# Moving three of the four token sums of each FFN into the output projection before it, and taking two gate columns fewer as whole products

## The chip, the cores and the metric

One core of a Trainium2 chip runs the whole program. The time is device time in microseconds of one execution, told as the median of several. The engines are TensorE (PE; its weight loads are PEld), VectorE (DVE), ScalarE (ACT), GpSimd (POOL) and SyncE (SP, which here only issues transfers). The granted TensorE clock in the profiled execution is 0.998.

## The reference

A decoder trunk with two layers over 512 tokens of width 1024, all in float32. Layer 0 mixes with a gated DeltaNet, layer 1 with sliding-window attention; both also attend into 256 memory tokens. What matters here is the end of each layer:

```
x = x + concat(mix_out, mem_o) @ w_out[layer]          # 1024 x 1024
gu = rms_norm(x, ln_ffn) @ w_gate_up[layer]            # 1024 x 5632
x = x + (silu(gu[:, :2816]) * gu[:, 2816:]) @ w_down[layer]
```

## The kernel before

**Tiles.** x is held transposed, as eight tiles x[0..7] of 128 features by 512 tokens. Each float32 operand is split in a high and a low part (`split`: ACT copies the high part, DVE subtracts it from the original), and a product is three matmuls, high by high, high by low and low by high (`mm3`). A weight column of 128 outputs is a 128x1024 tile: `load` (SP, 512 KB, two buffers `wraw`), then `weight` splits it into `whi` (ACT) and `wlo` (DVE), three buffers each. A whole column (`project`) is 8 x 3 matmuls of 128x512.

**Output projection** (`output`). Eight rows, one for each x[m]. Behind the last matmul of a row come, on DVE, `x <- pj,x` (add from PSUM), `l <- x,gains,h` (low part of the scaled row, after ACT's high part `h`) and `sqa <- sqa,sq` (sum of squares, after ACT's square). `opened_rows` gives a function `part(m, *ks)` that splits the weights of row m at its first call and runs some of its blocks k. The first three rows run in pieces beside the end of the mixer (`rest`); the other five follow one another in whole. In layer 0 the rows use blocks 6 and 7 (the memory heads `mq0`, `mq1`, held in the pool of layer 0) first.

**FFN** (`ffn`). A pair of columns for 512 tokens is taken in seven products of quarter size in place of eight (`quarters`: halves of the 1024 features against halves of the tokens, 4 x 3 matmuls of 128x256 each, 84 for a pair against 48 of 128x512 in two whole columns). It needs sums of weights and sums of activations. The weights: `s1` and `s3` are loaded by SP (lines 1112 and 1113) and a second quarter is added to each by an accumulating transfer issued by POOL (1114, 1115); the first column of the pair comes by `load`, the fourth quarter by line 1117. The activations: `token_sums(j)` for j = 0..3 combines x[j] and x[j+4]: on DVE one 128x256 `fs <- x,gains`, four 128x256 `fu <- x,...`, and the low halves of two 128x512 splits `T <- fu,T` (high halves on ACT). Products t1 to t4 of every pair need the sums of all four j; products 11, 21 and 22 need only h.

The four sums need all of x, so the first four gate columns of an FFN are taken whole while they are formed: gate 0, gate 1 (with the norm's reciprocal root between its matmuls), sums 0 and 1, gate 2, sums 2, gate 3, sums 3. Then follow pairs (`begin`): up 0-1, up 2-3, gate 4-5, up 4-5 and so on. The split halves of a product lie in a ring of six places that is cut out of the three `whi`/`wlo` buffers.

**Order.** The program text sets what depends on what. A planner lays out each engine's queue when the program is built: among the instructions that it holds to be ready, the one that the text emits first goes first. So an instruction of later text can stand in a queue before one of earlier text that is held to wait, and a later-emitted one that is ready stays behind an earlier-emitted one that is ready too. On the chip each queue runs in order. A tile that reuses a buffer waits for the last reader of the tile before it.

**Pools.** `fp` holds the FFN's tiles on the right side of the memory, where the mixer's pools were before; among them `T` (eight buffers, token sums), `ws` (s1 and s3), `fs`, `fu`. `xp` holds x and, under the tag `sq`, two buffers for squares.

Of the kernel before, what the change touches and what calls it, by code (L numbers as in the profile page):

```python
# [9 lines left out]
F32 = mybir.dt.float32  # L10
F32R = mybir.dt.float32r
# [7 lines left out]
P = 128  # L19
T = 512  # L20
D = 1024
KD = D // P
# [17 lines left out]
G_MIX, G_FFN, G_MEM, G_KV, G_FIN = (0, 8), (16, 24), 32, 40, 48  # L40
# [10 lines left out]
INV_FREQ = [float.fromhex(s) for s in (  # L51
    "0x1.0000000000000p+0", "0x1.8d275e0000000p-3", "0x1.3411900000000p-5", "0x1.ddee9c0000000p-8",
    "0x1.72ba440000000p-10", "0x1.1f91f00000000p-12", "0x1.be21880000000p-15", "0x1.5a0f4e0000000p-17")]
SHUFFLE = list(range(8, 16)) + list(range(8)) + list(range(16, 32))


# [31 lines left out]
class Builder:  # L88
    def __init__(self, tc, a):
        self.tc, self.nc, self.a = tc, tc.nc, a  # L90
        self.n = 0
        self.table, self.table_ins, self.table_users = None, None, []
        self.locked, self.latest = False, None


    def t(self, pool, shape, dtype=F32, tag=None, bufs=None, name=None):
# [158 lines left out]
    def build(self):  # L255
        tc, nc, a = self.tc, self.nc, self.a
        with ExitStack() as st:
            opened = lambda name, **kw: tc.tile_pool(name=name, bufs=1, reuse_waits="tile", **kw)
            pool = lambda name, **kw: st.enter_context(opened(name, **kw))
            cp = pool("const")  # L260
            self.wpool, self.apool = pool("w"), pool("acta")
            self.dpool = pool("scratch", space=DRAM)
            self.load_constants(cp)
            pool("edge", side="right").tile([P, 8], F32, name="edge")
            self.weng = nc.vector
            with opened("layer0", side="right") as self.mpool:
                with self.banks(pj=3, g=2, sc=3):
                    with opened("early", side="right") as ep:
                        self.mem_and_norm(ep)
                        self.gates(ep)  # L270
                    with opened("gdn", side="right") as gp:
                        mix, part = self.gdn(gp)
                    self.bpool, xp = pool("actb"), pool("x")
                    self.x = [self.t(xp, [P, T], F32, f"x{k}") for k in range(KD)]
                    for k in range(KD):
                        nc.sync.dma_start(self.x[k], a["xT"][:, k, :])
# [7 lines left out]
                    h = self.output(xp, 0, part, self.bpool, rest)  # L284
            with opened("ffn0", side="right") as fp, self.banks(pj=2, g=6):
                self.ffn(fp, xp, 0, h, self.apool, rope=True)
            with self.banks(pj=2, qk=1, pt=4):
                with opened("swa", side="right") as sp:
                    mix, rest = self.swa(sp, xp)
                    h = self.output(xp, 1, self.opened_rows(1, mix), self.apool, rest)  # L290
            with opened("ffn1", side="right") as fp, self.banks(pj=2, g=6):
                self.ffn(fp, xp, 1, h, self.bpool)

    def load_constants(self, cp):
        nc, a = self.nc, self.a
# [607 lines left out]
        return steps  # L903


    def row_bank(self, m):

        if m % 3 < 2:
            return self.bank("pj")
        if "g" in self.pbufs:  # L910
            return self.bank("g")
        return self.bank("qk", [P, 2, T])[:, 0]

    def opened_rows(self, layer, mix):

        rows = {}
# [12 lines left out]
    def output(self, xp, layer, part, hpool, ahead=None):  # L929

        nc, a = self.nc, self.a
        self.weng = nc.vector
        h = []
        self.acc = None

        def row(m, *ks):
            ps = part(m, *ks)
# [8 lines left out]
        if ahead is not None:  # L946
            ahead(row)
        for m in range(len(h), KD):
            row(m, 6, 7, 0, 1, 2, 3, 4, 5)
        return h  # L950

    def ffn(self, fp, xp, layer, h, apool, rope=False):

        nc, a = self.nc, self.a
        self.exact(xp)
        acc = self.acc
        acts, sums, open_pairs, places = [], [], [], []

        col = lambda f, up: a["wgu"][layer, 2 * f + up]

# [2 lines left out]
            self.use(SILU_SIN)  # L963

        def gate(f, between=None):
            return self.project(col(f, 0), h, "pj", between=between)

        def gated(ps):
            g = self.t(fp, [P, T], F32, "fg", 4)
            self.tt(nc.vector, g, ps, self.rstd, ALU.mult)  # L970
            self.fn(g, g, AF.Silu)
            return g
# [12 lines left out]
            places.append(places.pop(0))  # L985
            return places[-1]

        def begin(f, up, by, tag, bufs, then):

            o = [self.t(fp, [P, T], F32, tag, bufs) for _ in range(2)]  # L990
            steps = self.quarters(fp, [col(f + i, up) for i in range(2)], sums, by, o, ring)
# [60 lines left out]
        if tail < KD:  # L1052

            parts = (slice(0, T // 2), slice(T // 2, T))
            own = dict(pool=fp, tags=("T", "T"), bufs=8)
            w = {m: [down(m, j, n, **(own if m == KD - 1 else {})) for j, n in ((0, 6), (6, half - 6))] for m in range(tail, KD)}
            outs = [[self.t(fp, [P, D], F32, "T", 8).rearrange("p (k t) -> p k t", k=4) for _ in range(2)] for t in parts]
# [18 lines left out]
            for (ps, r), o, t in zip(ends, outs, parts):  # L1076
                self.store(ps, r, o, t)

    def token_sums(self, fp, layer, j, h):


        q = T // 2
# [6 lines left out]
        c = self.t(fp, [P, q], F32, "fs", 3)  # L1089
        raw = [self.t(fp, [P, T], F32, "fu", 3) for _ in range(2)]  # L1090
# [14 lines left out]
    def quarters(self, fp, src, sums, by, u, ring):  # L1105

        nc = self.nc
        q = T // 2
# [5 lines left out]
        nc.gpsimd.dma_start(s1, a22, accum_op=ALU.add)  # L1114
# [274 lines left out]
```

## Time and profile before

| | us |
|---|---|
| median of 3 runs | 1140.61 (1140.49 to 1140.86) |
| the profiled execution | 1140.3 |
| its span, first to last instruction | 1138.5 |
| PE busy | 1121.8 (99%) |
| DVE busy | 841.5 (74%) |
| ACT busy | 634.0 (56%) |
| POOL busy | 86.1 (8%) |

The span has 19673 instructions. A row of a timeline gives start, duration, engine, line, operation, what is written from what, and in brackets the idle time ahead of it with what ended that. A row of the chain gives start, duration and the work that stands on the path to the end of the span. A row of a window table gives a stretch, its length, and the busy time of each engine in it.

### The profile page before, as it was taken

What the parts mean: (1) busy time and instruction counts of PE and PEld (TensorE: products, weight loads), DVE (VectorE), ACT (ScalarE), POOL (GpSimd) and SP (SyncE); (2) the same over time, 40 slices, a digit from 0 to 9 for tenths busy, and PEclk for the clock granted to TensorE, in tenths of its full rate; (3) what the DMA queues carried; (4) which work ended last, traced back from release to release, by engine and by line L of the source; (5) the groups of instructions that cost most, each with busy time, mean ns of one, the idle gap of its engine ahead of it and who ended that gap; (6) DMA issues with size and microseconds to landing.
All of it is one profiled execution on the core that took longest, in us unless ns stands there. A gap on an engine that the chain in (4) does not pass through costs nothing.

```text
span 1138.5 us, 19673 instructions
## 1 busy us (share of the span) xinstructions
PE 1121.8 (99%) x7476; PEld 992.8 (87%) x7476; DVE 841.5 (74%) x1590; ACT 634.0 (56%) x1278; POOL 86.1 (8%) x97
## 2 busy tenths in 40 slices
PE   7999999999999999999999999999999999999997
PEld 6888887887899998899998888888999988999986
DVE  6754887776789987389876768959799843899743
ACT  7569572365566653256653656855566522566524
POOL 0120000000101100011100000010011100111000
PEclk9999999999999999999999999999999999999999
DMA  8433342324668744567723421153477833677232
GB/s 311 119 123 114 119 107 99 95 91 149 188 143 190 189 124 130 158 144 188 186 71 93 135 74 57 42 130 126 121 187 177 202 98 107 149 190 182 70 95 95
DMA packets 73971, 152.76 MB, mean 134 GB/s; under 512 B 17756, under 2 KB 18420, under 8 KB 73876
## 3 DMA queue, kind: packets, MB, share of 16 engines
q1 hardware_dynamic: 62356, 130.52, 37.4%
q0 software_dynamic: 11520, 20.98, 11.9%
q8 instruction: 59, 0.97, 0.3%
q14 instruction: 36, 0.29, 0.1%
HBM read 144.51 MB, written 6.96 MB: 133 GB/s over the span
## 4 chain that ended last, share of the span: by engine, by line
PE 95%; DVE 2%; ACT 1%; DMA 1%; issue 1%; SPq 0%; DVEq 0%; ACTq 0%
PE pj L154 48%; PE g L154 37%; PE sc L154 6%; PE pt L154 2%; PE qk L154 2%; PE pt L168 1%; PE g L168 1%; DVE wlo L171 1%; DMA wraw<-in_wmk 1%; ACT whi L148 0%; ACT sm L142 0%; SPq L329 0%; DVE x L171 0%; DVE l L174 0%; DVE stats L836 0%
## 5 line engine op out<-in xcount | busy, mean ns | idle before, releaser
L148 ACT ACTIVATE whi<-wraw 128x512 fp32r<-128x512 f32 (+2 forms) x331 | 243.6, 746 | 249.1 <-PE pj L154 160.1
L171 DVE TENSOR_TENSOR wlo<-wraw,whi 128x512 fp32r<-128x512 f32 (+2 forms) x331 | 273.0, 835 | 109.1 <-ACT whi L148 102.7
L154 PE MATMUL pj<-h,whi 128*128 128x512 f32 (+1 forms) x676 | 265.5, 393 | 0.1
L154 PE MATMUL pj<-l,whi 128*128 128x512 f32 (+1 forms) x676 | 263.7, 390 | 0.0
L154 PE MATMUL pj<-h,wlo 128*128 128x512 f32 (+1 forms) x676 | 263.2, 390 | 0.0
L154 PE MATMUL g<-T,whi 128*128 128x256 f32 x1280 | 228.1, 278 | 0.2
L154 PEld LDWEIGHTS g<-T,whi 128*128 128x128 f32 x1280 | 194.7, 188 | 1.8 <-DVE fu L174 1.8
L154 PE MATMUL g<-T,wlo 128*128 128x256 f32 x640 | 177.8, 278 | 0.0
L154 PEld LDWEIGHTS pj<-h,whi 128*128 128x128 f32 x676 | 126.9, 188 | 28.3 <-issue 3.5
L154 PEld LDWEIGHTS pj<-h,wlo 128*128 128x128 f32 x676 | 127.0, 188 | 25.9 <-DVE wlo L171 0.4
L154 PEld LDWEIGHTS pj<-l,whi 128*128 128x128 f32 x676 | 127.1, 188 | 24.7 <-DVE l L171 0.4
L154 PE MATMUL g<-h,whi 128*128 128x256 f32 (+1 forms) x492 | 138.4, 281 | 0.0
L154 PE MATMUL g<-h,wlo 128*128 128x256 f32 (+1 forms) x492 | 138.0, 280 | 0.0
L154 PE MATMUL g<-l,whi 128*128 128x256 f32 (+1 forms) x492 | 138.0, 280 | 0.0
L154 PEld LDWEIGHTS g<-T,wlo 128*128 128x128 f32 x640 | 120.1, 188 | 0.0
L154 PEld LDWEIGHTS g<-l,whi 128*128 128x128 f32 x492 | 92.3, 188 | 0.8 <-issue 0.2
L154 PEld LDWEIGHTS g<-h,whi 128*128 128x128 f32 x492 | 92.3, 188 | 0.8 <-issue 0.2
L154 PEld LDWEIGHTS g<-h,wlo 128*128 128x128 f32 x492 | 92.3, 188 | 0.5
L1114 POOL DMA_DIRECT2D ws<-in_wgu x40 | 35.5, 887 | 700.7 <-DMA ws<-in_wgu 278.2
L148 ACT ACTIVATE whi<-ws 128x512 fp32r<-128x512 f32 x80 | 50.5, 631 | 48.9 <-PE g L154 38.4
L171 DVE TENSOR_TENSOR wlo<-ws,whi 128x512 fp32r<-128x512 f32 x80 | 54.7, 684 | 4.5 <-ACT whi L148 4.5
L1115 POOL DMA_DIRECT2D ws<-in_wgu x40 | 35.1, 877 | 213.4 <-DVE wlo L171 73.5
(383 smaller groups left out, 1637.4 us busy)
## 6 DMA issues: line engine op xcount, KB each, us to landing
wraw<-in_wgu SPq DMA_DIRECT2D x48, 512.0 KB, 4.2
ws<-in_wgu SPq DMA_DIRECT2D x80, 256.0 KB, 3.5
ws<-in_wgu POOLq DMA_DIRECT2D x80, 256.0 KB, 4.8
wraw<-in_wdn SPq DMA_DIRECT2D x48, 384.0 KB, 3.1
wraw<-in_win SPq DMA_DIRECT2D x26, 512.0 KB, 3.6
wraw<-in_wgu SPq DMA_DIRECT2D x40, 256.0 KB, 4.4
wraw<-in_wout SPq DMA_DIRECT2D x16, 512.0 KB, 3.6
wraw<-in_wdn SPq DMA_DIRECT2D x16, 256.0 KB, 2.7
```

Of the source, the lines that this page charges most:

```text
L148: self.copied = self.nc.scalar.activation(out, in_, AF.Copy, **kw).ins
L154: return self.chained(self.nc.tensor.matmul(out, lhsT, rhs, start=start, stop=stop, skip_group_check=more).ins)
L168: return self.chained(self.nc.tensor.transpose(out, in_, self.ident[:k, :k]).ins)
L171: return eng.tensor_tensor(out=out, in0=a, in1=b, op=op).ins
L1114: nc.gpsimd.dma_start(s1, a22, accum_op=ALU.add)
L1115: nc.gpsimd.dma_start(s3, a21, accum_op=ALU.add)
```

## The change

It has five parts.

1. The rows of the output projection are taken in the order 0, 4, 1, 5, 2, 6, 3, 7 (`TURN`), so that x[j] and x[j+4] come one behind the other. r counts in this order; the gate columns run through the blocks of h in the same order.
2. Behind the rows r = 3, 4 and 6 the weights of row r + 1 are opened (`part(r + 1)` with no blocks: load and split only), and then the token sums 0, 1 and 2 are emitted. Their temporaries come from a pool `turn` that lives in `output` and from the tag `sq` of `xp`; their results lie in a pool `tok` that lives on (six buffers `T`), and `fp` keeps two `T` for the fourth sum. The `T` tiles of the last FFN's end are taken from both.
3. Only gate 0 and gate 1 are whole columns. Sum 3 is emitted behind them. Gate 2-3 becomes a pair in quarters.
4. s1, s3 and the fourth quarter of the first pair (`summed`) are emitted before the norm's results are used, and the load of that pair's first column is held behind them in SP's queue (`behind`, an order without a wait).
5. `token_sums` gets its temporaries and pool from the caller; `quarters` takes quarters already loaded.

```diff
+TURN = (0, 4, 1, 5, 2, 6, 3, 7)
     def load(self, src, pool=None, bufs=2):
-        self.nc.sync.dma_start(raw, src)
+        ins = self.nc.sync.dma_start(raw, src).ins
+        if self.behind is not None:
+            self.nosync(ins, self.behind)
+            self.behind = None
...
+                    self.tok = pool("tok")
...
-        def part(m, *ks):
-            if m not in rows:
-                rows[m] = self.weight(self.a["wout"][layer, m]), self.row_bank(m), []
-            w, ps, done = rows[m]
+        def part(r, *ks):
+            if r not in rows:
+                rows[r] = self.weight(self.a["wout"][layer, TURN[r]]), []
+            if not ks:
+                return
+            if r not in banks:
+                banks[r] = self.row_bank(r)
+            (w, done), ps = rows[r], banks[r]
...
+        def work():
+            return self.t(xp, [P, T], F32, "sq", 2)[:, :T // 2], [self.t(tp, [P, T], F32, "raw", 2) for _ in range(2)]
+
+        def row(r, *ks):
+            ps = part(r, *ks)
             if ps is None:
                 return
+            m = TURN[r]
             self.tt(nc.vector, self.x[m], ps, self.x[m], ALU.add)
-            hl = self.pair(hpool)
-            self.split_gain(self.x[m], self.gain(G_FFN[layer], m), *hl)
-            h.append(hl)
+            h[m] = self.pair(hpool)
+            self.split_gain(self.x[m], self.gain(G_FFN[layer], m), *h[m])
             self.acc = self.accumulate(xp, self.acc, self.x[m])
+            if r in (3, 4, 6):
+                part(r + 1)
+                sums.append(self.token_sums(layer, len(sums), h, work, self.tok, 6))
...
         def gate(f, between=None):
-            return self.project(col(f, 0), h, "pj", between=between)
+            return self.project(col(f, 0), h, "pj", TURN, between=between)
...
-            whole = []
+            whole, loaded = [], None
             if f0 == 0:
                 two = [gate(0), gate(1, {1: [norm]})]
+                loaded = self.summed(fp, columns(0, 1))
+                self.behind = self.quarter
                 whole += [gated(ps) for ps in two]
-                sums += [self.token_sums(fp, layer, f, h) for f in range(2)]
-                for f in (2, 3):
-                    whole.append(gated(gate(f)))
-                    sums.append(self.token_sums(fp, layer, f, h))
+                sums.append(self.token_sums(layer, 3, h, work, fp, 2))
...
-                begin(f, 1, g, "fu", 3, put)
+                begin(f, 1, g, "fu", 3, put, loaded)
+                loaded = None
...
-        hl = [self.t(fp, [P, D], F32R, "T", 8) for _ in range(2)]
+        hl = [self.t(pool, [P, D], F32R, "T", bufs) for _ in range(2)]
...
+    def summed(self, fp, src):
         (a11, a12), (a21, a22) = ([c[:, :T], c[:, T:]] for c in src)
-        a1 = self.load(src[0])
         s1, s3 = (self.t(fp, [P, T], F32, "ws", 4) for _ in range(2))
         nc.sync.dma_start(s1, a21)
         nc.sync.dma_start(s3, a11)
         nc.gpsimd.dma_start(s1, a22, accum_op=ALU.add)
         nc.gpsimd.dma_start(s3, a21, accum_op=ALU.add)
         last = self.t(fp, [P, T], F32, "wraw", 2)
-        nc.sync.dma_start(last, a22)
+        self.quarter = nc.sync.dma_start(last, a22).ins
+        return s1, s3, last
+
+    def quarters(self, fp, src, sums, by, u, ring, loaded=None):
+        a1 = self.load(src[0])
+        s1, s3, last = loaded or self.summed(fp, src)
```

More of the change, by code (lines that the diff above doesn't have):

```diff
@@ L92, in __init__ @@
         self.table, self.table_ins, self.table_users = None, None, []
-        self.locked, self.latest = False, None
+        self.locked, self.latest, self.behind = False, None, None
     def t(self, pool, shape, dtype=F32, tag=None, bufs=None, name=None):
@@ L282, in rest @@
                                 row(m, k)
-                    h = self.output(xp, 0, part, self.bpool, rest)
+                    h, sums = self.output(xp, 0, part, self.bpool, rest)
             with opened("ffn0", side="right") as fp, self.banks(pj=2, g=6):
-                self.ffn(fp, xp, 0, h, self.apool, rope=True)
+                self.ffn(fp, xp, 0, h, sums, self.apool, rope=True)
             with self.banks(pj=2, qk=1, pt=4):
@@ L289, in build @@
                     mix, rest = self.swa(sp, xp)
-                    h = self.output(xp, 1, self.opened_rows(1, mix), self.apool, rest)
+                    h, sums = self.output(xp, 1, self.opened_rows(1, mix), self.apool, rest)
             with opened("ffn1", side="right") as fp, self.banks(pj=2, g=6):
-                self.ffn(fp, xp, 1, h, self.bpool)
+                self.ffn(fp, xp, 1, h, sums, self.bpool)
     def load_constants(self, cp):
@@ L914, in opened_rows @@
     def opened_rows(self, layer, mix):
-        rows = {}
-        def part(m, *ks):
-            if m not in rows:
-                rows[m] = self.weight(self.a["wout"][layer, m]), self.row_bank(m), []
-            w, ps, done = rows[m]
+        rows, banks = {}, {}
+        def part(r, *ks):
[6 more added lines that the diff above has]
+            (w, done), ps = rows[r], banks[r]
             for k in ks:
@@ L932, in output, with ffn @@
         self.weng = nc.vector
-        h = []
+        h, sums = {}, []
         self.acc = None
-        def row(m, *ks):
-            ps = part(m, *ks)
+        def work():
+            return self.t(xp, [P, T], F32, "sq", 2)[:, :T // 2], [self.t(tp, [P, T], F32, "raw", 2) for _ in range(2)]
+        def row(r, *ks):
+            ps = part(r, *ks)
             if ps is None:
                 return
+            m = TURN[r]
             self.tt(nc.vector, self.x[m], ps, self.x[m], ALU.add)
-            hl = self.pair(hpool)
-            self.split_gain(self.x[m], self.gain(G_FFN[layer], m), *hl)
-            h.append(hl)
+            h[m] = self.pair(hpool)
+            self.split_gain(self.x[m], self.gain(G_FFN[layer], m), *h[m])
             self.acc = self.accumulate(xp, self.acc, self.x[m])
[L946 to L952, printed above, removed]
+            if r in (3, 4, 6):
+                part(r + 1)
+                sums.append(self.token_sums(layer, len(sums), h, work, self.tok, 6))
+        with self.tc.tile_pool(name="turn", bufs=1, reuse_waits="tile") as tp:
+            if ahead is not None:
+                ahead(row)
+            for r in range(len(h), KD):
+                row(r, 6, 7, 0, 1, 2, 3, 4, 5)
+        return h, sums
+    def ffn(self, fp, xp, layer, h, sums, apool, rope=False):
         nc, a = self.nc, self.a
@@ L956, in ffn @@
         acc = self.acc
-        acts, sums, open_pairs, places = [], [], [], []
+        acts, open_pairs, places = [], [], []
         col = lambda f, up: a["wgu"][layer, 2 * f + up]
@@ L965, in gate, with work @@
         def gate(f, between=None):
-            return self.project(col(f, 0), h, "pj", between=between)
+            return self.project(col(f, 0), h, "pj", TURN, between=between)
+        def work():
+            return self.t(fp, [P, T // 2], F32, "fs", 3), [self.t(fp, [P, T], F32, "fu", 3) for _ in range(2)]
         def gated(ps):
@@ L986, in ring, with columns, begin @@
             return places[-1]
-        def begin(f, up, by, tag, bufs, then):
+        def columns(f, up):
+            return [col(f + i, up) for i in range(2)]
+        def begin(f, up, by, tag, bufs, then, loaded=None):
             o = [self.t(fp, [P, T], F32, tag, bufs) for _ in range(2)]
-            steps = self.quarters(fp, [col(f + i, up) for i in range(2)], sums, by, o, ring)
+            steps = self.quarters(fp, columns(f, up), sums, by, o, ring, loaded)
             next(steps)
@@ L1077, in ffn, with token_sums @@
                 self.store(ps, r, o, t)
-    def token_sums(self, fp, layer, j, h):
+    def token_sums(self, layer, j, h, work, pool, bufs):
         q = T // 2
@@ L1088, in token_sums @@
         x0, x1 = self.x[j], self.x[j + 4]
-        c = self.t(fp, [P, q], F32, "fs", 3)
-        raw = [self.t(fp, [P, T], F32, "fu", 3) for _ in range(2)]
+        c, raw = work()
         t = [x[:, i * q:(i + 1) * q] for x in raw for i in range(2)]
```

13 lines of the change are left out of this document (7 added, 6 removed).

## The prediction

> **What bounds the kernel now.** First the page: its head, the busy line of TensorE, and the shares of the chain of work that ended last.
>
> ```profile
> span 1138.5 us, 19673 instructions
> PE 1121.8 (99%) x7476; PEld 992.8 (87%) x7476; DVE 841.5 (74%) x1590; ACT 634.0 (56%) x1278; POOL 86.1 (8%) x97
> ...
> PE 95%; DVE 2%; ACT 1%; DMA 1%; issue 1%; SPq 0%; DVEq 0%; ACTq 0%
> ```
>
> TensorE is on 95% of the chain, so time comes only from fewer or cheaper matmuls, or from its pauses. Then the chain in order of time, which gives the pace of both kinds of matmul; "x66" counts them.
>
> ```profile
> 312.79 14.98 PE pj L154 x66
> 327.77 96.60 PE g L154 x828
> ...
> 772.18 5.44 PE qk L154 x24
> ...
> 795.76 15.00 PE pj L154 x66
> 810.76 96.60 PE g L154 x828
> ```
>
> A 128x512 matmul of a whole column takes 14.98 / 66 = 0.227 us (a column or row of 24: 5.44), a 128x256 one of the quarters 96.60 / 828 = 0.1167 us. The row at 772.18 is r5 of layer 1. Both stretches lie on the chain without a gap, in both layers: the whole gates run straight into the quarters.
>
> Third, the windows cut at the rows and columns of layer 0: r4, r5, r6, r7, and gate 1 (gate 0 fills the 5.44 us between).
>
> ```profile
> core 0: us, PE busy (x) PEld busy (x) DVE busy (x) ACT busy (x) POOL busy (x), PEclk, DMA share, GB/s
> 283.93:289.21 5.28, 5.28 (x23) 4.40 (x24) 3.60 (x5) 3.25 (x4) 0.00 (x0) 1.00 0.59 189
> 289.21:294.65 5.44, 5.44 (x25) 4.50 (x25) 3.87 (x5) 2.34 (x4) 0.00 (x0) 1.00 0.47 127
> 294.65:300.10 5.45, 5.45 (x25) 4.51 (x25) 3.18 (x4) 2.20 (x4) 0.00 (x0) 1.00 0.60 195
> 300.10:305.54 5.44, 5.44 (x25) 4.50 (x25) 5.19 (x10) 2.31 (x4) 1.01 (x1) 1.00 0.50 147
> ...
> 310.98:316.89 5.91, 5.91 (x27) 4.87 (x27) 5.91 (x11) 4.58 (x6) 1.25 (x2) 1.00 0.99 177
> ```
>
> TensorE never pauses here. VectorE is the nearest rival: in the four rows it idles 1.68 + 1.57 + 2.27 + 0.25 = 5.77 us. Whether the moved sums fit there decides the result.
>
> **The change part by part.**
>
> *Gates 2 and 3 in quarters.* Removed on TensorE: 48 x 0.227 = 10.90 us. Added: 84 x 0.1167 = 9.80. Gain 1.10 us for each FFN, less some 0.02 for the hand-over of a pair: 1.07, and **2.14 us for both**. The pair also moves 5 x 256 KB + 512 KB where two columns moved 1 MB, by two more SP issues and two more POOL issues, and VectorE work of the kind of the ten pairs of this window:
>
> ```profile
> 327.77:424.37 96.60, 96.60 (x830) 96.60 (x829) 86.42 (x156) 61.27 (x118) 13.00 (x16) 1.00 0.71 170
> ```
>
> 86.42 of 96.60 us on VectorE, 61.27 on ScalarE, 0.71 of the DMA engines: an eleventh pair like these is hidden, zero. If VectorE were the limit there, a pair would cost 8.64 us of it, which TensorE's 9.66 still covers.
>
> *Three token sums beside the rows.* Pace of VectorE by starts of neighbours, layer 0:
>
> ```profile
> 276.26 0.69 DVE L171 TENSOR_TENSOR x<-pj,x 128x512 f32<-128x512 f32 x1 [2.24 <-PE pj L154]
> 277.13 1.22 DVE L171 TENSOR_TENSOR wlo<-wraw,whi 128x1024 fp32r<-128x1024 f32 x1 [0.18 <-ACT whi L148]
> 278.27 0.68 DVE L171 TENSOR_TENSOR x<-pj,x 128x512 f32<-128x512 f32 x1
> 278.87 0.74 DVE L174 SCALAR_TENSOR_TENSOR l<-x,gains,h 128x512 fp32r<-128x512 f32 x1
> 279.53 0.68 DVE L171 TENSOR_TENSOR x<-g,x 128x512 f32<-128x512 f32 x1
> ...
> 283.89 0.69 DVE L171 TENSOR_TENSOR x<-pj,x 128x512 f32<-128x512 f32 x1
> 285.01 1.23 DVE L171 TENSOR_TENSOR wlo<-wraw,whi 128x1024 fp32r<-128x1024 f32 x1 [0.43 <-ACT whi L148]
> ...
> 305.16 0.48 DVE L174 SCALAR_TENSOR_TENSOR fu<-x,gains,fs 128x256 f32<-128x256 f32 x1
> 305.56 0.48 DVE L174 SCALAR_TENSOR_TENSOR fu<-x,eps,fu 128x256 f32<-128x256 f32 x1
> ...
> 308.21 0.68 DVE L171 TENSOR_TENSOR sqa<-sqa,sq 128x512 f32<-128x512 f32 x1
> 308.82 0.68 DVE L171 TENSOR_TENSOR T<-fu,T 128x512 fp32r<-128x512 f32 x1
> 309.42 0.48 DVE L174 SCALAR_TENSOR_TENSOR fu<-x,gains,fs 128x256 f32<-128x256 f32 x1
> ...
> 313.16 0.34 DVE L178 TENSOR_SCALAR fs<-x,gains 128x256 f32<-128x256 f32 x1
> 313.42 1.21 DVE L171 TENSOR_TENSOR wlo<-wraw,whi 128x1024 fp32r<-128x1024 f32 x1
> ```
>
> So wlo 1.14, x 0.60, l 0.66, sqa 0.60, fu 0.40, T 0.60, fs 0.26. A token sum is 0.26 + 4 x 0.40 + 2 x 0.60 = 3.06 us; a row is 0.60 + 0.66 + 0.60 + 1.14 = 3.00. A row that carries a sum needs 6.06 us and has 5.44. Rows r4 and r5 carry sums 0 and 1; r6 carries none, r7 has sum 2. The third matmul of a row needs its wlo, 2 x 0.227 = 0.45 us after the row starts.
>
> Replay of layer 0 from 283.89, the queue in the order of the text wherever things are ready: x3, l, sqa, the additions of sum 0 and its first T take 0.60 + 0.66 + 0.60 + 1.86 + 0.60 = 4.32, to 288.2. Then the second T, or wlo of r5 (emitted after them). Layer 1 shows which, and how its first rows stand:
>
> ```profile
> 759.37 1.37 DVE L171 TENSOR_TENSOR x<-pj,x 128x512 f32<-128x512 f32 x2 [0.93 <-PE pj L154]
> 760.65 1.22 DVE L171 TENSOR_TENSOR wlo<-wraw,whi 128x1024 fp32r<-128x1024 f32 x1
> ...
> 765.59 1.21 DVE L171 TENSOR_TENSOR wlo<-wraw,whi 128x1024 fp32r<-128x1024 f32 x1
> ...
> 777.82 0.68 DVE L171 TENSOR_TENSOR T<-fu,T 128x512 fp32r<-128x512 f32 x1
> 778.42 0.48 DVE L174 SCALAR_TENSOR_TENSOR fu<-x,gains,fs 128x256 f32<-128x256 f32 x1
> 778.82 0.68 DVE L171 TENSOR_TENSOR x<-qk,x 128x512 f32<-128x512 f32 x1
> 779.42 0.68 DVE L171 TENSOR_TENSOR T<-fu,T 128x512 fp32r<-128x512 f32 x1
> ```
>
> Between the two T of one sum (777.82, 779.42) other work is let in, since the second waits for ScalarE's high half. I take wlo of r5 to go there: 288.2 to 289.4, due at 289.21 + 0.45 = 289.66, no pause. The second T ends at 289.95; x4, sum 1 without its last T, l, sqa and wlo of r6 take 0.60 + 2.46 + 0.66 + 0.60 + 1.14 = 5.46, to 295.4, due 294.65 + 0.45 = 295.10: **0.3 us late**. r6 has no sum and gives 2.4 us back, so r7, gate 0 and gate 1 are in time. In layer 1 wlo of r4 starts at 765.59 and ends at 766.73; the same sum puts wlo of r6 at 766.73 + 4.32 + 1.14 + 0.60 + 5.46 = 778.25, due a row and 0.45 after 772.18, at 778.07: **0.2 late**. If each split stands behind both T, r5 is 0.3 late and r6 some 0.6 more; if the next x add slips ahead as well, 1.5 in all for a layer. Bounds 0 and 3.0 for both layers; I take 0.5, the replay's order, since the rows of layer 1 show it.
>
> *Rows in the order 0, 4, 1, 5.* In layer 0 x is loaded during these very rows. The view of that line's transfers, the issues of x[4] and x[5] alone:
>
> ```profile
> L276 SPq DMA_DIRECT2D x<-in_xT x2: 376/403/430, 274.5 to 274.9; - x2
> ...
> DMA to landing us min/median/max: 6.1/6.2/6.3
> ```
>
> x[4] lands at 274.5 + 6.1 = 280.6. The second row's add stood at 278.27 with x[1]; with x[4] it can't run before 280.6, and all behind it in VectorE's queue waits, wlo of r4 among them, which TensorE wants at about 283.7. The load order isn't changed. Bounds: 280.6 - 278.27 = **2.3 us** if the add keeps its place, 0 if r2's add and other ready work are laid ahead of it. The planner seems to know late landings: in layer 1 the first two adds stand together (759.37, x2) ahead of wlo, in layer 0 wlo comes between them (277.13). So I take 0.5, nearer the lower end. Layer 1 has x in place: 0.
>
> *Sum 3, gates 0 and 1.* From 305.54: x 0.60, l 0.66, sqa 0.60, the split of the squares' sum 0.60, wlo of both gates 2.28, sum 3 3.06, two gate products 1.20 and the first four splits of quarters with their added weights, 5 x 0.60: 12.0 us, against 11.35 to the quarters' start at 316.89 and 7 products' time beyond; the last ones are due only then. Zero; uncovered, up to 0.6 once in each layer.
>
> *Added weights earlier, the pair's first column behind them.* SP and POOL do the same issues some 10 us earlier against the columns. The tiles may now lie on memory held for the last row's blocks 6 and 7 (in use to 300.10 + 6 x 0.227 = 301.5). From there a load, an accumulation and two splits:
>
> ```profile
> 303.35 1.01 POOL L1114 DMA_DIRECT2D ws<-in_wgu  x1 [238.09 <-DMA ws<-in_wgu]
> ...
> DMA to landing us min/median/max: 2.6/4.7/7.7
> ```
>
> With the median landing twice, 301.5 + 4.7 + 1.0 + 4.7 + 1.2 = 313.1; with the longest, 319.1. Due 316.89 + 12 x 0.1167 + 0.23 = 318.5. Zero, at worst 0.6 in layer 0; the held load of 512 KB has until 316.89 too.
>
> [...]
>
> **Sum.** -2.14 + 0.5 + 0.5 = -1.1 us. The profiled execution took 1140.3 (span 1138.5), 0.3 below the median of 1140.61; against the median this is **1139.5**. A difference of 0.2%, 2.28 us, is about what a measurement of this kernel can tell from no change.
>
> **Rivals.** *Nothing late* (chance 0.22): all splits fall in gaps and x[4] waits beside other work; 1140.61 - 2.14 = 1138.5, and a little less, to 1138.0, if the new order also fills the small waits ahead of r4. For it: 5.77 us of idle VectorE. Against it: 6.06 in 5.44 for two rows. Rather more than half of it, 0.13, lies past 0.2%.
>
> *x[4] or the splits take the gain back* (0.30): 2.3 for x[4] with the replay's 0.5, or 1.0 to 1.5 late in each layer, or 0.6 more where the longest landing delays the first added weights: -2.14 + 2.0 to -2.14 + 3.0, so 1140.4 to 1141.5. For it: the landing at 280.6. Against it: the order shown at 277.13.
>
> *Slower: VectorE's queue lets the sums ahead of every split* (0.10). Three sums are 9.18 us against 5.77 idle, 3.4 late at gate 0 in a layer, with x[4] 2.3 more: -2.14 + 6.8 + 2.3 = +7.0, 1147.6 at the far end; it decides from 4.4 us of pauses in both layers, 1142.9, on. Against it: the row without a sum, and the gaps between two T.
>
> *The first half shows no gain* since quarters become bound by VectorE: -2.14 is lost, 1141.6; 8.64 against 9.66 speaks against it (counted with the second rival).
>
> My forecast, 1138.9 to 1140.3, holds the rest, 0.38. Range 1138.1 to 1142.0. Faster 0.13, same 0.77, slower 0.10.
>
> **What would show it.** The chain after: two whole columns (some 40 matmuls) ahead of the quarters in place of four, and a first stretch of quarters of 96.6 + 9.8 = 106.4 us. r4 to r7 at 5.44 us each, with a pause at r6's third matmul of about 0.3. x <- pj,x of the second row at 280.6 or later. First quarters without a wait for ws. The forecast is wrong if pauses of TensorE between 278 and 317, or between 760 and 800, sum to over 2 us, or if the quarters' pace leaves 0.1167.

## The result, and the profile after

The changed kernel takes **1157.2 us** (1156.96 to 1157.48, 4 runs) against 1140.55 in the runs beside it (1140.39 to 1140.86): ratio 1.0146, 95% interval 1.0133 to 1.0158. It is slower by 16.65 us where 1.1 us of gain was forecast.

The head and the busy line of the page, then the longest pieces of the chain (start, length, work):

```profile
span 1155.5 us, 19874 instructions
...
PE 1124.7 (97%) x7548; PEld 998.6 (86%) x7548; DVE 850.1 (74%) x1612; ACT 640.9 (55%) x1294; POOL 90.0 (8%) x101
```

```profile
328.91 103.87 PE g L155 x888
434.97 64.61 PE pj L155 x285
499.58 93.83 PE g L155 x805
...
815.50 108.77 PE g L155 x912
926.45 64.63 PE pj L155 x285
```

In layer 0 the first down projection began at 427.16 and now begins at 434.97 (+7.81); the quarters behind it moved from 491.32 to 499.58 (+8.26). In layer 1 the two places moved from 910.15 to 926.45 (+16.30) and from 974.31 to 991.08 (+16.77), so layer 1 adds 8.5 of its own. Each FFN should have been 1.07 faster, so each lost some 9.3 to 9.6 us up to its second run of quarters. The rows of the output projection did not lose it. Windows over r4 to r7 of layer 0 and over the rows and columns of layer 1 (length, then PE, PEld, DVE, ACT, POOL):

```profile
284.00:305.90 21.90, 21.90 (x98) 18.03 (x97) 20.86 (x36) 12.38 (x19) 0.00 (x0) 1.00 0.25 80
...
770.00:808.00 38.00, 38.00 (x167) 31.08 (x166) 33.40 (x57) 20.32 (x31) 1.75 (x2) 1.00 0.39 119
```

TensorE has no pause in either. VectorE fills 20.86 of 21.90 us, where three rows with a sum and one without were put at 3 x 6.06 + 3.00 = 21.2, and it is enough. The loss begins behind gate 1. Layer 0, rows of VectorE, SyncE, GpSimd, ScalarE and TensorE in this order:

```profile
308.76 0.68 DVE L172 TENSOR_TENSOR T<-raw,T 128x512 fp32r<-128x512 f32 x1
...
309.47 0.33 SPq L1132 DMA_DIRECT2D ws<-in_wgu  x1
...
312.69 0.56 SPq L1137 DMA_DIRECT2D wraw<-in_wgu  x1
...
313.20 1.01 POOL L1134 DMA_DIRECT2D ws<-in_wgu  x1 [248.04 <-DMA ws<-in_wgu]
...
312.81 1.15 ACT L149 ACTIVATE T<-fu 128x512 fp32r<-128x512 f32 x2 [1.15 <-DVE fu L175]
321.23 0.63 ACT L149 ACTIVATE whi<-ws 128x512 fp32r<-128x512 f32 x1 [7.26 <-DMA ws<-in_wgu]
321.76 1.13 ACT L149 ACTIVATE whi<-wraw 128x512 fp32r<-128x512 f32 x2
322.80 0.67 ACT L143 ACTIVATE rstd<-g,eps 128x512 f32<-128x512 f32 x1
...
328.49 0.37 ACT L149 ACTIVATE fs<-g 128x256 f32<-128x256 f32 x1
...
322.43 0.58 PE L155 MATMUL g<-h,whi 128*128 128x256 f32 x1 [5.30 <-ACT whi L149]
...
328.91 0.51 PE L155 MATMUL g<-T,whi 128*128 128x256 f32 x2 [0.61 <-ACT fs L149]
```

Read it as one chain. VectorE reads `raw` of sum 2 for the last time until 309.44; 0.03 us later SyncE issues the load of s1, and seven more loads follow within 3.8 us (2.5 MB in all, called the burst below). s1 is there at 313.2, the accumulation onto it lands at 321.2. ScalarE has had nothing to do since 313.9, because `whi <- ws` stands next in its queue; behind that stand the split of the first product's own weights, the norm's reciprocal root, gate 0's activation and, at 328.49, the copy `fs` that frees a bank for the third product. TensorE waits 5.3 us for the first product and 0.61 for `fs`. Between the two it runs at half clock, a granted clock of 0.50 (the column behind POOL's):

```profile
318.00:320.00 2.00, 0.00 (x0) 0.00 (x0) 0.00 (x0) 0.00 (x0) 0.00 (x0) 1.00 1.06 234
320.00:322.00 2.00, 0.00 (x0) 0.00 (x0) 0.11 (x1) 0.77 (x2) 0.86 (x1) 0.95 1.02 230
322.00:324.00 2.00, 1.56 (x5) 1.26 (x6) 2.00 (x4) 1.97 (x4) 0.85 (x1) 0.50 0.89 160
324.00:326.00 2.00, 2.00 (x12) 2.00 (x11) 1.59 (x3) 1.97 (x4) 0.00 (x0) 0.50 1.00 140
...
328.00:330.00 2.00, 1.39 (x11) 1.10 (x11) 1.71 (x3) 2.00 (x5) 0.86 (x1) 0.84 0.31 31
```

Without a wait the third product starts 24 x 0.1167 = 2.8 us behind gate 1, at about 319.8 (gate 1 ended at 316.9 as before). It starts at 328.91: 9.1 us, the loss of the layer. In layer 1 `raw` is last read until 800.28, the load is issued at 800.31, the accumulation lands at 811.8, gate 1 has ended at 808.2, and the first quarter starts at 815.50, again at half clock (pieces of the chain, then the window of its first 24 matmuls):

```profile
800.31 2.78 DMA ws<-in_wgu
803.64 8.17 DMA ws<-in_wgu
811.84 0.63 ACT whi L149
```

```profile
815.50:820.50 5.00, 5.00 (x24) 5.00 (x25) 3.15 (x6) 2.44 (x5) 0.00 (x0) 0.54 0.54 105
```

Why SyncE waits at all is seen in the addresses of the built program (bytes in a partition): s1, placed on memory of a closed pool, waits for the last read there, and is issued 0.03 us behind it in both layers.

```
raw, two buffers of pool turn       173504 .. 177600   last read by sum 2
changed kernel: s1                  175040 .. 177088   first use ahead of fg
fg_first:       s1                  183232 .. 185280   first use behind fg
```

Only s1 lies on `raw`; in the built program its load waits for VectorE's last `T <- raw,T`. s3 lies further on in both kernels, but its load stands behind that of s1 in SyncE's queue.

### The profile page after: what moved, and what is told of

It reads as the page before. It is cut to its first block, busy times and chain, and to the rows that moved or that the text cites. A ratio compares the mean times of both kernels' runs of the same rounds, so it can differ in the third digit from the quotient of the medians.

```text
span 1155.5 us, 19874 instructions
## 1 busy us (share of the span) xinstructions
PE 1124.7 (97%) x7548; PEld 998.6 (86%) x7548; DVE 850.1 (74%) x1612; ACT 640.9 (55%) x1294; POOL 90.0 (8%) x101
## 4 chain that ended last, share of the span: by engine, by line
PE 65%; DVE 3%; DMA 1%; ACT 1%; issue 0%; DVEq 0%; POOLq 0%; ACTq 0%
PE g L155 35%; PE pj L155 26%; PE pt L155 2%; PE qk L155 1%; DVE wlo L172 1%; PE pt L169 1%; DMA ws<-in_wgu 1%; DVE T L172 0%; DMA wraw<-in_wout 0%; DVE x L172 0%; DVE l L175 0%; ACT sm L143 0%; ACT whi L149 0%; DVE raw L175 0%; DVE sqa L172 0%
## 5 line engine op out<-in xcount | busy, mean ns | idle before, releaser
L155 PE MATMUL pj<-h,whi 128*128 128x512 f32 (+1 forms) x644 | 253.2, 393 | 0.1
L155 PE MATMUL pj<-l,whi 128*128 128x512 f32 (+1 forms) x644 | 251.4, 390 | 0.0
L155 PE MATMUL pj<-h,wlo 128*128 128x512 f32 (+1 forms) x644 | 250.8, 390 | 0.0
L155 PE MATMUL g<-T,whi 128*128 128x256 f32 x1344 | 241.9, 280 | 0.8 <-ACT fs L149 0.6
L155 PEld LDWEIGHTS g<-T,whi 128*128 128x128 f32 x1344 | 206.1, 189 | 2.4 <-DVE fu L175 1.5
L155 PE MATMUL g<-T,wlo 128*128 128x256 f32 x672 | 187.6, 279 | 0.0
L155 PE MATMUL g<-h,whi 128*128 128x256 f32 (+1 forms) x516 | 146.5, 284 | 12.6 <-ACT whi L149 12.6
L155 PE MATMUL g<-h,wlo 128*128 128x256 f32 (+1 forms) x516 | 146.0, 283 | 0.0
L155 PE MATMUL g<-l,whi 128*128 128x256 f32 (+1 forms) x516 | 145.8, 283 | 0.0
L155 PEld LDWEIGHTS pj<-h,whi 128*128 128x128 f32 x644 | 120.9, 188 | 27.0 <-issue 3.5
L155 PEld LDWEIGHTS pj<-h,wlo 128*128 128x128 f32 x644 | 121.0, 188 | 24.6 <-DVE wlo L172 0.4
L155 PEld LDWEIGHTS pj<-l,whi 128*128 128x128 f32 x644 | 121.1, 188 | 23.6 <-DVE l L175 0.4
L155 PEld LDWEIGHTS g<-T,wlo 128*128 128x128 f32 x672 | 127.0, 189 | 0.0
L155 PEld LDWEIGHTS g<-h,whi 128*128 128x128 f32 x516 | 97.8, 190 | 14.2 <-ACT whi L149 13.5
L155 PEld LDWEIGHTS g<-l,whi 128*128 128x128 f32 x516 | 97.9, 190 | 0.8 <-issue 0.2
L155 PEld LDWEIGHTS g<-h,wlo 128*128 128x128 f32 x516 | 97.9, 190 | 0.8 <-DVE wlo L172 0.3
```

The source lines that it names most:

```text
L155: return self.chained(self.nc.tensor.matmul(out, lhsT, rhs, start=start, stop=stop, skip_group_check=more).ins)
```

## The experiments

Medians in us; the interval is that of the ratio to the kernel before (1140.4 to 1140.7 beside each).

| kernel | median (lowest to highest) | ratio, 95% |
|---|---|---|
| changed | 1157.2 (1156.96 to 1157.48) | 1.0146 (1.0133 to 1.0158) |
| fg_first | 1141.4 (1140.14 to 1141.93) | 1.0007 (0.9998 to 1.0016) |
| no_behind | 1151.53 (1151.02 to 1153.68) | 1.0100 (1.0086 to 1.0114) |
| whole_four | 1141.24 (1140.41 to 1142.02) | 1.0006 (0.9998 to 1.0015) |
| fg_first_x | 1139.63 (1139.12 to 1142.16) | 0.9994 (0.9985 to 1.0003) |
| sum2_early | 1156.31 (1155.82 to 1157.55) | 1.0140 (1.0126 to 1.0154) |
| idle_matmuls | 1162.04 (1161.64 to 1163.03) | 1.0191 (1.0178 to 1.0205) |
| whole_four_x | 1140.42 (1139.81 to 1141.24) | 1.0001 (0.9993 to 1.0010) |
| summed_between | 1139.63 (1138.77 to 1140.22) | 0.9992 (0.9983 to 1.0000) |
| norm_first | 1152.67 (1151.08 to 1153.9) | 1.0105 (1.0091 to 1.0119) |
| sum2_norm | 1149.13 (1147.52 to 1150.13) | 1.0075 (1.0062 to 1.0087) |
| norm_idle | 1157.36 (1152.63 to 1158.46) | 1.0141 (1.0123 to 1.0160) |
| fg_first_x_norm | 1138.6 (1138.38 to 1139.06) | 0.9983 (0.9975 to 0.9992) |
| sum2_norm2 | 1146.84 (1145.01 to 1148.31) | 1.0057 (1.0044 to 1.0071) |

**fg_first: only the place of ws.**

```diff
                 two = [gate(0), gate(1, {1: [norm]})]
+                whole += [gated(ps) for ps in two]
                 loaded = self.summed(fp, columns(0, 1))
                 self.behind = self.quarter
-                whole += [gated(ps) for ps in two]
```

> The changed kernel with two lines swapped: gate 0's and gate 1's products (fg) are emitted ahead of summed, so that fg and not s1 and s3 lie at the foot of the FFN's pool, over the 2.5 KB that it shares with the pool turn. Theory memory (s1 waits until sum 2 has read raw, at 309.5 and 800.3): s1 is issued some 8 us earlier, no pause at the first quarter, the whole loss of 9.1 + 9.7 us goes: 1138.4, within 0.7. Rival accumulation (POOL's transfers land late since VectorE or the queues are full, however early s1 is): still over 1150. Rival order (the pair's first column is held behind the added weights): no change from 1157, since that order stays.

The queues of all five engines hold the same instructions in the same order as the changed kernel's, and those of TensorE, VectorE and ScalarE the same waits too; only waits on the transfer queues (SyncE, GpSimd) differ, among them the one for VectorE ahead of s1. So the 15.8 us between 1157.2 and 1141.4 are those of the place in memory. Its timeline:

```profile
301.06 0.42 SPq L1132 DMA_DIRECT2D ws<-in_wgu  x1
...
306.50 1.01 POOL L1134 DMA_DIRECT2D ws<-in_wgu  x1 [240.97 <-DMA wraw<-in_wgu]
...
314.05 0.62 ACT L149 ACTIVATE whi<-ws 128x512 fp32r<-128x512 f32 x1
315.61 0.67 ACT L143 ACTIVATE rstd<-g,eps 128x512 f32<-128x512 f32 x1
...
321.72 0.50 PE L155 MATMUL g<-T,whi 128*128 128x256 f32 x2 [1.63 <-ACT fs L149]
```

s1 is issued 8.4 us sooner, its accumulation lands in 4.7 us, and `whi <- ws` now runs without idle time ahead of it. The time is 3.0 above the 1138.4 expected; a pause of 1.63 us at the third product is more than half of that.

**no_behind: the load of the pair's first column free to go ahead.**

```diff
-                self.behind = self.quarter
```

> The changed kernel without the order that holds the pair's first column behind the added weights; s1 still lies on turn's memory. Theory memory: s1 is still issued at about 309.5 and 800.3 and its split stands ahead of the first product's in ScalarE's queue, so the pause stays; the burst behind s1 is 1 MB smaller and ends perhaps 2 to 4 us earlier in each layer: 1149 to 1154. Rival order: the pause goes, 1139.

5.7 us back. s1 is issued at 309.45 as before, but two loads fewer lie in the burst behind it: the accumulation issued at 313.43 is there at 318.2, after 4.8 us in place of 8.0. The queue changed as well: with its column loaded earlier, the first product's own splits stand ahead of `whi <- ws` (at 306.62 and 314.44 in layer 0), and that product follows gate 1 without a pause. What each of the two is worth is not separated. TensorE still waits for `fs`, 4.09 us in layer 0 and 1.98 in layer 1.

**whole_four: gates 2 and 3 whole again.**

```diff
-                self.behind = self.quarter
...
+                whole += [gated(gate(f)) for f in (2, 3)]
+                self.behind = self.quarter
```

> The changed kernel with gates 2 and 3 whole again, between sum 3 and the first quarters; sums 0 to 2 stay in the output rows, s1 stays on turn's memory. Theory memory: s1 is as late as before, but two columns (10.9 us) cover it: no pause, 1140.5 within 1.0, the time before the change. Rival rows (the sums in the output rows cost pauses of TensorE): 1142 or more. Rival accumulation: as theory memory.

s1 lies on raw's memory and the added weights land at 320.9, as late as in the changed kernel, but two columns, 10.9 us, stand ahead of its use: `328.97 96.60 PE g L155 x828` in the chain, no wait for ws. The late landing alone costs nothing; it is the new use that comes too soon. One other pause is left in layer 0, at the last block of gate 0, where VectorE's `l` of the last row is late: `311.30 0.50 PE L155 MATMUL pj<-l,whi 128*128 128x512 f32 x1 [0.78 <-DVE l L175]`.

**fg_first_x: x loaded in the order of its use as well.**

```diff
-                    for k in range(KD):
+                    for k in TURN:
                         nc.sync.dma_start(self.x[k], a["xT"][:, k, :])
```

> As the kernel with fg first, and x is loaded in the order of the rows (0, 4, 1, 5, ...) in layer 0. If x[4]'s landing holds up VectorE (2.3 us in my bounds), 0.5 to 2.3 us faster than with fg first alone; if other work is laid ahead of that add, the same within 0.3.

1.8 us faster than fg_first, within what was expected if x[4] holds VectorE up; but the queues are laid anew too (`whi <- ws` runs at 311.74 in place of 314.05), and the two are not separated. Layer 0 is clean now (s1 issued at 293.57; first quarters `316.61 106.40 PE g L155 x912`); 0.6 us of small pauses are left at the first quarters of layer 1.

**whole_four_x and summed_between.** The first is whole_four with that order of x, the second is fg_first_x with the fetch of the added weights emitted between gate 0 and gate 1.

> Sums behind rows and weights ahead as changed, but gates 2 and 3 whole columns again (emitted between sum 3 and the first quarters), and x loaded in the order 0, 4, 1, 5, 2, 6, 3, 7. Beside fg_first_x it lacks only the seven products for gates 2 and 3. If these are worth what the matmuls say, 1.07 for each FFN, it is 2.1 slower than fg_first_x: about 1141.0 to 1142. Rival (fg_first_x owes its time to the order of x alone): within 0.5 of fg_first_x.

> fg_first_x with the fetch of the first added weights emitted between gate 0 and gate 1, so that SyncE issues it ahead of gate 1's load, and the load of the pair's first column no longer tied behind anything of gate 1's. If the remaining pauses of fg_first_x in layer 1 (0.6 us by the first quarters) come of weights that land late, it is 0.5 faster than fg_first_x; if they come of ScalarE's and VectorE's order, it is the same within 0.3.

whole_four_x stands at 1140.42, its chain nearly piece for piece that of the kernel before (quarters from 327.77 and 810.80 on, for 327.77 and 810.76). The pause of 0.78 us is gone, so the order of x was worth 0.8 there. fg_first_x is only 0.8 faster, not 2.1; small pauses take back part of the rest. summed_between is as fg_first_x, but it tests little: its s1 is issued where that of fg_first_x is (294.21 for 293.57, 777.03 for 776.65), so the edit did not move the fetch. That the weights are not late shows in fg_first_x itself, where `whi <- ws` of layer 1 runs at 794.97 without idle time ahead of it.

**sum2_early: raw's memory free 5 us sooner.**

```diff
-            if r in (3, 4, 6):
+            if r in (3, 4, 5):
```

> The changed kernel with the third token sum one row earlier (behind r = 5 in place of 6), so that the last read of raw, and with it the release of the memory on which ws lies, comes one row, about 5.4 us, sooner in each layer. Memory theory (the loads of s1 and s3 wait for the last read of raw, and the whole rest of the delay follows from that): SyncE issues them near 304 in place of 309.5 in layer 0, the pause ahead of the first quarters shrinks from 5.7 to near 0.3, and the half clock behind it goes too; 9.1 - 1 to 2 is won back in layer 0 and about as much in layer 1, some 1141 to 1146 in all; a third row in succession with a sum may cost up to 1 us a layer. Rival (the accumulation by GpSimd, or the order of ScalarE's queue, is slow wherever it starts): no more than 2 us are won back, 1155 to 1158.

```profile
304.14 0.33 SPq L1132 DMA_DIRECT2D ws<-in_wgu  x1
...
315.69 0.63 ACT L149 ACTIVATE whi<-ws 128x512 fp32r<-128x512 f32 x1 [6.18 <-DMA ws<-in_wgu]
316.23 0.61 ACT L149 ACTIVATE whi<-wraw 128x512 fp32r<-128x512 f32 x1
316.75 1.13 ACT L149 ACTIVATE T<-fu 128x512 fp32r<-128x512 f32 x2
...
318.31 0.67 ACT L143 ACTIVATE rstd<-g,eps 128x512 f32<-128x512 f32 x1
...
326.03 0.79 PE L155 MATMUL g<-T,whi 128*128 128x256 f32 x2 [4.45 <-ACT fs L149]
```

1141 to 1146 was expected, and it takes 1156.3. The load does start 5.3 us sooner and the first quarter starts at gate 1's end. But only 0.9 us is won: the accumulation, among eight loads again, takes 7.8 us, ScalarE still stands for 6.18 us at `whi <- ws`, and here even the high parts of sum 3 (`T <- fu`) are queued behind it, so VectorE idles too (0.00 us busy in 312 to 316, 0.60 in 316 to 318); the wait reappears at the third product. What counts in both kernels is not when the first product needs ws, but when ScalarE's queue comes to it, at about 309.5 here and 313.9 in the changed kernel.

**idle_matmuls: the pause filled with work that nobody reads.** 24 matmuls of gate 1 once more behind gate 1.

> The changed kernel with 24 more 128x512 matmuls behind gate 1 in each FFN: gate 1's product once more, into a PSUM bank that nothing reads. They fill 5.4 us of the pause in which TensorE waits for the first added weights. Clock theory (the pause itself lowers the granted clock, so that the first quarters run at 0.21 us in place of 0.117): the pause is no shorter in sum, but the first quarters run at 0.117, which wins back about 2.3 us in layer 0 and 2.0 in layer 1: about 1153, 1152 to 1154.5. Rival (the quarters' slow start comes of late operands or of the accumulating transfers, not of the pause): 1156.5 or more.

4.8 us slower, against the expectation. The first quarters do run at full clock, but the wait for `fs` that the slow clock had covered comes forth (4.39 us, for 0.61 in the changed kernel), and half clock with it:

```profile
329.94 0.80 PE L155 MATMUL g<-T,whi 128*128 128x256 f32 x2 [4.39 <-ACT fs L149]
```

```profile
322.00:326.00 4.00, 3.54 (x27) 3.09 (x25) 3.06 (x6) 3.94 (x6) 0.86 (x1) 1.00 0.92 164
326.00:330.00 4.00, 0.07 (x1) 0.07 (x1) 2.68 (x5) 2.64 (x7) 0.86 (x1) 0.82 0.16 49
330.00:334.00 4.00, 4.00 (x19) 4.00 (x20) 2.40 (x4) 1.58 (x4) 0.00 (x0) 0.50 1.01 272
```

So in layer 0 of the changed kernel half clock was not the bound: ScalarE's chain from `whi <- ws` to `fs`, 7.3 us, was. The run shows when half clock comes, not what it costs.

**norm_first: ready work ahead of `whi <- ws` in ScalarE's queue.**

```diff
...
             self.split(raw, *w)
+            if loaded and b == "11":
+                self.early.append(self.copied)
+            if loaded and b == "t1":
+                for u in self.early:
+                    self.nosync(self.copied, u)
```

`early` holds gate 0's activation, the last high part of sum 3 and the split of the first product.

> The changed kernel with one order added in ScalarE's queue, in each FFN: the high part of the first added weights (whi <- ws) stands behind the norm's reciprocal root, gate 0's activation, the high parts of the fourth sum and of the first quarter's own weights. Nothing else moves; ws still waits for raw's memory and lands as late. Queue theory (about half of the loss is work that was ready and stood behind whi <- ws): the first product starts right behind gate 1, the second with the landing, and no wait for fs follows; 3.6 to 4.9 us back in layer 0, 5 to 6.4 in layer 1: 1146 to 1149. Rival (the landing alone sets the pause): at most 1.4 us, one product, back in each layer: 1154.4 to 1157.

4.5 us back, between the two: in the profiled execution 1.6 in layer 0, about what the rival allows (1.4), and 4.7 in layer 1. In layer 0 the reciprocal root comes only at 318.12, behind two splits that wait for the pair's first column, and `whi <- ws` only at 322.37. Its waits on TensorE, and the clock in layer 1 behind pauses of at most 1.23 us:

```profile
323.04 0.79 PE L155 MATMUL g<-T,whi 128*128 128x256 f32 x2 [3.13 <-ACT whi L149]
...
811.02 0.50 PE L155 MATMUL g<-T,whi 128*128 128x256 f32 x2 [1.23 <-ACT whi L149]
```

```profile
812.00:814.00 2.00, 1.64 (x14) 1.64 (x15) 1.88 (x4) 2.00 (x5) 0.86 (x1) 1.00 0.68 118
```

**norm_idle: norm_first with 12 matmuls in the pause.**

> norm_first with 12 more 128x512 matmuls behind gate 1 in each FFN (gate 1's first four blocks once more, into a bank that nothing reads): 2.7 us of work within the pause, which leaves under 2 us of pause at a time. Clock theory (a pause of several us makes the next quarters run at half clock, 0.21 us a matmul): 1.3 us for each layer whose pause in norm_first was followed by half clock, so 1 to 3 us faster than norm_first. Rival (late operands set that pace): equal to norm_first or slower.

4.7 us slower than norm_first. Its rows show waits for `fs` again (2.5 us in two): with other matmuls the planner laid other splits ahead of that copy. It changed two things and settles nothing on the clock.

**sum2_norm and sum2_norm2: free memory and queue together.** The second adds `"t2"` to the condition, so that the second product's second split stands behind the root as well.

> Both in one: the third sum a row earlier, so that raw's memory comes free 5 us sooner, and the order of norm_first in ScalarE's queue. If the two causes together are the whole loss, the first quarters run without a pause over 1 us, the first products at 0.117 us a matmul: 1139 to 1142. Rival (a third cause, such as the accumulating transfers under the burst of loads): 1145 or more.

> sum2_norm with the second product's second split as well (the high part of the pair's first column after s1 is added to it) behind the norm's reciprocal root and gate 0's activation. In sum2_norm the root still stood behind that split, which waits for ws as whi <- ws does, and ran at 316.7 and 804.6 with pauses of 1.9 and 3.1 us and half clock behind them. Queue theory (with memory free early, what is left of sum2_early's loss is only ready work behind instructions that wait for ws): no pause over 1 us, 1139.5 to 1142. Rival (the accumulation lands too late in the burst of loads whatever the queue): 1145 or more.

1149.1 and 1146.8: both miss what was expected and lie where their rivals put them, at 1145 or more. The rows of the first that show why, ScalarE in layer 0:

```profile
316.14 0.63 ACT L149 ACTIVATE whi<-wraw 128x512 fp32r<-128x512 f32 x1 [3.21 <-DVE wraw L172]
316.68 0.67 ACT L143 ACTIVATE rstd<-g,eps 128x512 f32<-128x512 f32 x1
```

The root stood behind a second instruction that waits for ws by way of VectorE. In sum2_norm2 the root runs at 312.83 and 798.36, but gate 0's product now stands behind such an instruction in VectorE's queue, and with the added order `whi <- ws` waits for it:

```profile
801.57 0.69 DVE L172 TENSOR_TENSOR wraw<-ws,wraw 128x512 f32<-128x512 f32 x1 [2.75 <-DMA ws<-in_wgu]
...
803.51 0.68 DVE L172 TENSOR_TENSOR fg<-pj,rstd 128x512 f32<-128x512 f32 x1
```

So the rows of sum2_early, sum2_norm and sum2_norm2 show the same thing in a new place: a queue that comes early to a user of ws stops there, and ready work behind it is late. It is not the whole of it. The landing leaves little room as well: in layer 1 the accumulation, issued at 792.74 among eight loads, takes 8.7 us and lands at 801.5, as gate 1 ends. No run separates its part from the queue's. sum2_norm2's pauses at the first quarters are 0.97 us in layer 0 and 2.31 in layer 1, each with 0.4 of small ones, 4.1 together; 1140.3 - 2.1 + 4.1 would be 1142.3, its profiled execution takes 1145.0, and its runs reach 1148.3. Of that rest 0.5 is a pause at the rows of layer 1, where now three rows in succession carry a sum; what is left of it stays open.

**fg_first_x_norm: the version that beats both.** fg_first_x with norm_first's order.

> The fastest version so far (ws on other memory, x loaded in the order 0, 4, 1, 5, 2, 6, 3, 7) with the order of norm_first in ScalarE's queue. It has 0.6 us of small pauses left at the first quarters of layer 1: 1139.1, 1138.5 to 1139.7. Rival (those come of other work, or the order delays a split of another product): as fg_first_x or up to 2 us slower.

1138.6 us, 1.9 faster than the kernel before, the interval clear of 1, and the pauses of fg_first_x at the first quarters of layer 1 are gone. Its chain:

```profile
317.04 106.42 PE g L155 x912
...
798.77 106.53 PE g L155 x912
```

## Why the prediction was wrong, point by point

**The step that failed is "Added weights earlier ... Zero, at worst 0.6 in layer 0".** It failed in three places.

1. *When the memory is free.* The step took the memory of blocks 6 and 7, free at 301.5, as what the tiles may lie on. s1 lies on `raw` of the pool `turn`, which the same change brought in, and that is read until 309.44 in layer 0 and 800.28 in layer 1. The chain came out 8.0 later at this point; the load took less than put in (from 309.47 to the accumulation's issue 3.7, for 4.7 + 1.0), the accumulation more (8.0 for 4.7; it goes out with the burst that the same wait had held back, and in fg_first, where the eight loads go out over 8.6 us, it takes 4.7). 313.1 + 8.0 - 2.0 + 3.3 = 322.4, where the first quarter is found (322.43). The step put layer 1 at zero and gave no reason for it; the same `raw` made it the dearer one (its first 24 matmuls end at 820.5; without a wait it would be at 808.2 + 2.8 = 811.0, 9.5 us sooner).
2. *What it costs to be late.* Due was put at 318.5, so 322.4 would have cost 3.9. It cost 9.1, for the wait cost all that stood behind it in ScalarE's queue: ScalarE came to `whi <- ws` at 313.9, and root, activation and `fs` behind it set the third product at 328.91. sum2_early shows this apart from the memory.
3. *Half clock* behind the pause was not priced. Where it bounds, in layer 1, 24 matmuls take 5.0 us (815.50 to 820.50, mean clock 0.54) in place of 2.8.

A busy VectorE as the cause of the late landing, one half of the rival accumulation put up for fg_first, is not borne out by this trace: in layer 1 the accumulation issued at 803.64 took 8.2 us with VectorE idle from 804.9 to its landing at 811.8, in layer 0 8.0, from 313.2 to 321.2, with VectorE idle from 314.8. With fewer loads beside it the landing came sooner (no_behind, 4.8).

**The other steps.** *Gates 2 and 3 in quarters, -2.14*: right. The forecast stretch of 106.4 us is 106.42 and 106.53 in fg_first_x_norm, and that kernel is 1.9 faster than the one before and 1.8 faster than whole_four_x, which has gates 2 and 3 whole and no pause there. *Three sums beside the rows, +0.5*: too dear; the windows over the rows show no pause in either layer. *x[4], +0.5*: the replay was right in kind. The planner lays r2's work ahead of the add that is late:

```profile
278.72 0.69 DVE L172 TENSOR_TENSOR x<-g,x 128x512 f32<-128x512 f32 x1
279.32 0.74 DVE L175 SCALAR_TENSOR_TENSOR l<-x,gains,h 128x512 fp32r<-128x512 f32 x1
279.98 1.22 DVE L172 TENSOR_TENSOR wlo<-wraw,whi 128x1024 fp32r<-128x1024 f32 x1
281.13 0.69 DVE L172 TENSOR_TENSOR x<-pj,x 128x512 f32<-128x512 f32 x1
```

The add runs at 281.13, later than 280.6 as said, with wlo of r4 ahead of it, and costs nothing in the changed kernel: the lower end. In whole_four the order of x is worth the 0.8 us above, between the bounds. *Sum 3 and the gates, zero*: 8.54 of 10.70 us of VectorE in the columns' window of 306.0 to 316.7 would have allowed it, and in the changed kernel sum 3 is done at 314.8. Only the products of gates 0 and 1, counted in the same step, came late (324.31 and 327.24), behind the root in ScalarE's queue. *The rival that ended slower* named the wrong queue: the sums ahead of the splits on VectorE, not ws ahead of the root on ScalarE. *The signs*: a wait of the first quarters for ws and a pace other than 0.1167 are what the trace shows. The windows named for the pauses, 278 to 317 and 760 to 800, show none over 0.1 us: the pauses stand just behind them, at 317.1 and 808.2.

## What to carry to other kernels

When a change opens a pool and moves a fetch ahead, look up on whose memory the fetched tile lies, with the pool that the change itself adds: its first free moment is the last read of what lay there (here 309.44, with s1 issued at 309.47), and an early issue is worth nothing before it. Then price a late operand not by its first user's due time but by the moment at which an in-order queue reaches it, and by all the ready work behind it there. Moving the tile (two lines) was worth 15.8 us; freeing the memory sooner without looking at the queues was worth 0.9.

## What the runs showed of the hardware

How long half clock lasted can be estimated from the mean clocks of the windows, if the clock is 1.00 or 0.50 throughout. In layer 0 of the changed kernel (0.95 in 320 to 322, 0.84 in 328 to 330 above) it lasted from 321.8 to 328.64, 6.84 us; in layer 1 (0.83 in 812 to 814, 0.96 in 820 to 822) from 813.3 to 820.2, 6.8; in layer 0 of sum2_norm (0.74 in 321 to 322, 0.55 in 324 to 325), where a pause of 1.94 us ends at 320.53, from 321.5 to 324.9, 3.4.

At the first quarters it came in or behind each of these pauses of 3.1 us and more: 3.10 (sum2_norm, layer 1), 3.13 (norm_first), 4.09 (no_behind, at 0.21 us a matmul), 4.39 (idle_matmuls), 4.45 and 4.6 (sum2_early), 5.30 and 7.33 (changed kernel). Of the pauses about 2 us long, it came with 1.94 (sum2_norm) and 2.23 (norm_idle, 0.75 in 322 to 323), and not with 1.98 (no_behind, layer 1, on at 0.117 us a matmul) and 2.31 (sum2_norm2, 1.00 from 804 to 812). In layer 1 of norm_idle it began behind two pauses of 1.44 and 0.83 close together (1.00 in 812 to 814, 0.50 in 814 to 816); with a single 1.63 (fg_first) and with 1.23 and smaller ones around it (norm_first, layer 1) the clock stayed at 1.00. So a pause of about 2 us can be enough here, though not always; what decides it is shown by no run.

An accumulating transfer of 256 KB onto s1 took from 3.7 to 9.7 us from issue to landing in the changed kernel (42 of them), its median 4.5; the first ones of each FFN, in the burst of eight loads, 8.0 and 8.2.
